# Modulation rows of both halves turned together, experts' weight pieces ending at banks, tokens gathered one expert at a time

## The chip, the cores and the metric

The kernel runs on one core of a Trainium2 chip. The metric is the device time of one execution in microseconds (us). Engines are named as in the profile: PE is TensorE's matmuls and PEld its loads of the stationary operand, DVE is VectorE, ACT is ScalarE, POOL is GpSimd, and SP issues most of the transfers.

## What is computed

The reference takes 256 tokens of width 1024 through two blocks of two layers each, all in float32. Two parts of it matter here. The first block modulates its activations by six rows per layer that come from the conditioning vectors:

```python
mod = silu_c @ ada_w[l] + ada_b[l]
modc = silu_cc @ ada_w[l] + ada_b[l]
sh1, sc1, g1, sh2, sc2, g2 = [m[:, None, :] for m in jnp.split(mod, 6, axis=-1)]
...
a = modulate(h, norm1_g[l], sh1, sc1)     # rmsnorm(h, g) * (1 + scale) + shift
```

The last layer of the second block is a mixture of 8 experts of hidden width 1408. Each token goes to its two best experts; an expert computes `(silu(h @ w1) * (h @ w3)) @ w2`, and the results are added with the router's weights.

## The kernel before

The weights, some 400 MB of float32, are read once, in the order in which they are used. `wload` (L225 to L236) moves a piece of up to 2048 columns by 128 rows into a buffer `raw` (SP issues the transfer at L225). It then handles sub-pieces of up to 1024 columns: ACT casts one to the rounded format fp32r, `whi` (L233), and DVE subtracts this from the raw piece to get the low part `wlo` (L236); in the experts' stage every sixth `wlo` is POOL's. The tokens are split in the same way (`xh`, `xl`; `gh`, `gl` for gathered tokens). A product of full precision is then three fp32r matmuls that add into one bank of 512 columns: `gemm_tok` issues high times high (L326), high times low (L327) and low times high (L328) for each group of 128 rows and each bank; such three are a triple below. The buffers are rings: a transfer waits until the slot it will fill has been read.

The experts' w1 and w3 have 1408 columns, which `cut` divides into banks of 512, 512 and 384. They are the only weights here wider than 1024, so for them `plan` lays 8 rows of 1408 end to end and cuts the whole at every 2048 columns, and `wload` at every 1024. These cuts fall inside banks, and a bank cut in two costs two triples of its row group.

The modulation's rows are made in `ada`, a generator that the kernel steps along between other work. For each layer, each of six rows s and each half h of 512 columns, PE computes the row (L509, a stationary operand of 32 columns), ACT copies the result from its bank to a tile `mod` (L516), and PE turns it from a row into a column per group of 128 features (L520): 8 matmuls whose stationary operand is every eighth column of `mod`, 64 columns in all, and whose moving operand is a selector of 2 columns (`c_sel`). In float32 each is two matmul instructions, so the trace has 16 in a run. DVE adds the bias and applies the norm's gain (L521, L524). There are 24 such halves. Those of the first two rows come first of all; while their weights arrive, `busy` (L473) fills PE's row with matmuls on zeros. The others are stepped in the background of the first block's GEMMs.

`moe` (L1700) first ranks the tokens of each expert, and splits the token state into `xth` and `xtl` (written at L373). `gather` (L1787) then makes a one-hot matrix `G` on DVE for two experts together (L1790, compared with a row of indices, `b_iota`). For each of 8 feature groups k it multiplies `G`, 256 columns wide, with every eighth column of `xth` and `xtl` (L1798), and the results are copied to `gh` by ACT and to `gl` by DVE (L1801). The first gather runs alone; the later ones are stepped in the background of the GEMMs, as are `weigh` (L1811, the weights of an expert's tokens, `cmb`), `turn` (L1831) and `scatter` (L1838). For an expert come w1, then the w2 of the expert before it, whose evacuation is `yh` and `yl` (L1862), then w3. A GEMM takes its banks from a ring of four.

Of the kernel before, what the change touches and what calls it, by code (L numbers as in the profile page):

```python
# [10 lines left out]
F32 = mybir.dt.float32  # L11
F32R = mybir.dt.float32r
# [3 lines left out]
OP = mybir.AluOpType  # L16
# [68 lines left out]
class Net:  # L85
# [134 lines left out]
    def wload(self, src, n, cw, f0):  # L220
# [5 lines left out]
        step = 1024 if len(src.shape) == 2 else 1024 // cw * cw  # L226
        out = []
        for c in range(0, n, step):
            m = min(step, n - c)
            s = raw[:, c:c + m]  # L230
# [7 lines left out]
            for k in range(a // cw, -(-(a + m) // cw)):  # L238
                o = k * cw - a
                out.append((k, max(0, -o), min(cw, m - o), *((lambda c, n, d=d, o=o: d[:, o + c:o + c + n]) for d in (hi, lo))))  # L240
        return out

    @staticmethod
    def plan(w, c0, cw):

        k, out = 0, []
        for view in w:
            nk = view.shape[1]
            if cw > 1024:
                flat = view.rearrange("p k n -> p (k n)")  # L250
                for f in range(0, nk * cw, 2048):
                    v = flat[:, f:min(f + 2048, nk * cw)]
                    out.append((repr(v), (v, v.shape[1], cw, k * cw + f)))
            else:
# [195 lines left out]
    def ada_setup(self):  # L450
        nc, a = self.nc, self.a
        self.zero = self.b1.tile([P, 512], BF16, name="zero")
        nc.vector.memset(self.zero, 0.0)
        self.ct = self.b1.tile([P, KD, 32], F32, name="ct")
# [14 lines left out]
    def busy(self, n):  # L469

        o = self.acc()
        for _ in range(n):
            self.tc.keep_in_program_order(self.nc.tensor.matmul(o, self.zero[:, :P], self.zero, start=True, stop=True))  # L473

    def ada_lambda(self):
# [4 lines left out]
        lqk = self.b1.tile([P, 2, 2, 64], F32, name="lqk")  # L480
# [12 lines left out]
    def ada(self, l, s, norm=None):  # L493
# [5 lines left out]
        self.mods[l, s] = o  # L499
        for h in range(2):  # L500
# [20 lines left out]
            nc.vector.tensor_tensor(out=o[rw], in0=pf[rw, :2 * KD].rearrange("p (k c) -> p k c", c=2),  # L521
                                    in1=self.adab[rw, l, s].unsqueeze(2).to_broadcast([64, KD, 2]), op=OP.add)
            if norm is not None:
# [1478 lines left out]
```

## Time and profile before

| | us |
|---|---|
| median of 3 runs | 2471.06 (2470.54 to 2473.48) |
| the profiled execution | 2465.78 |
| its span in the trace | 2464.3 |
| mean granted TensorE clock in it | 0.969 of full speed |
| busy in the span: PE, PEld, DVE, ACT, POOL | 2353.4, 1903.9, 1493.5, 1064.8, 299.0 |
| the experts' stage, first GEMM to last | 2000.9 to 2430.9 |

A busy share of the whole span says little here, since the stages have different limits: the page's slices show DVE between 2 and 8 tenths. Matmul records overlap their neighbours, as one is pipelined behind the other; the pace of PE is read from the starts of neighbours. The trace's instructions of `gemm_tok` in the experts' stage are known by `gh` and `gl`.

### The profile page before, as it was taken

What the parts mean: (1) busy time and instruction counts of PE and PEld (TensorE: products, weight loads), DVE (VectorE), ACT (ScalarE), POOL (GpSimd) and SP (SyncE); (2) the same over time, 40 slices, a digit from 0 to 9 for tenths busy, and PEclk for the clock granted to TensorE, in tenths of its full rate; (3) what the DMA queues carried; (4) which work ended last, traced back from release to release, by engine and by line L of the source; (5) the groups of instructions that cost most, each with busy time, mean ns of one, the idle gap of its engine ahead of it and who ended that gap; (6) DMA issues with size and microseconds to landing.
All of it is one profiled execution on the core that took longest, in us unless ns stands there. A gap on an engine that the chain in (4) does not pass through costs nothing.

```text
span 2464.3 us, 33187 instructions
## 1 busy us (share of the span) xinstructions
PE 2353.4 (95%) x13174; PEld 1903.9 (77%) x13174; DVE 1493.5 (61%) x2476; ACT 1064.8 (43%) x1684; POOL 299.0 (12%) x242
## 2 busy tenths in 40 slices
PE   8899999999998999999999989989999979999996
PEld 4567887777786778977887768868887778888885
DVE  4248732332356564568566765567566778897887
ACT  3137432222234544433343344423353447676773
POOL 1100000000002010003101210022101222222221
PEclk8899999999999999999999999999999989999998
DMA  8571244444323055544243444634343439888994
GB/s 296 150 201 52 88 151 144 159 166 163 107 81 123 10 200 164 196 147 156 84 160 130 154 165 148 215 111 143 102 161 120 155 129 346 292 327 288 328 337 159
DMA packets 121507, 419.45 MB, mean 170 GB/s; under 512 B 10992, under 2 KB 16112, under 8 KB 100352
## 3 DMA queue, kind: packets, MB, share of 16 engines
q1 hardware_dynamic: 114128, 401.32, 46.8%
q0 software_dynamic: 4832, 15.34, 2.3%
q8 instruction: 105, 1.72, 0.3%
q10 hardware_dynamic: 2384, 0.59, 0.1%
q14 instruction: 58, 0.48, 0.1%
HBM read 416.15 MB, written 1.07 MB: 169 GB/s over the span
## 4 chain that ended last, share of the span: by engine, by line
PE 84%; DVE 9%; issue 2%; ACT 2%; POOL 1%; DMA 1%; SPq 0%; ACTq 0%; POOLq 0%; DVEq 0%
PE acc L326 18%; PE acc L327 18%; PE acc L328 18%; PE acc L359 4%; PE acc L360 3%; PE acc L361 3%; DVE wlo L236 3%; PE mi L1032 2%; PE mi L520 2%; PE mi L509 2%; PE mi L1350 2%; PE mi L379 1%; PE mi L1798 1%; PE mi L988 1%; PE mi L1016 1%
## 5 line engine op out<-in xcount | busy, mean ns | idle before, releaser
L236 DVE TENSOR_TENSOR wlo<-raw,whi 128x1024 fp32r<-128x1024 f32 (+2 forms) x648 | 802.1, 1263 | 507.4 <-ACT whi L233 505.0
L233 ACT CAST whi<-raw 128x1024 fp32r<-128x1024 f32 (+2 forms) x692 | 673.0, 1010 | 741.5 <-PE acc L328 541.8
L326 PE MATMUL acc<-whi,xh 128*128 128x512 f32 (+3 forms) x1184 | 466.0, 397 | 18.6 <-ACT whi L233 12.4
L327 PE MATMUL acc<-wlo,xh 128*128 128x512 f32 (+3 forms) x1184 | 461.7, 390 | 11.9 <-DVE wlo L236 11.8
L328 PE MATMUL acc<-whi,xl 128*128 128x512 f32 (+3 forms) x1184 | 458.6, 388 | 3.4 <-DVE xl L373 3.4
L326 PEld LDWEIGHTS acc<-whi,xh 128*128 128x128 f32 x1184 | 227.9, 193 | 68.2 <-ACT whi L233 13.4
L327 PEld LDWEIGHTS acc<-wlo,xh 128*128 128x128 f32 x1184 | 227.8, 192 | 57.1 <-DVE wlo L236 19.8
L328 PEld LDWEIGHTS acc<-whi,xl 128*128 128x128 f32 x1184 | 227.7, 192 | 43.3 <-DVE xl L373 5.3
L326 PE MATMUL acc<-whi,hh 128*128 128x512 f32 x528 | 209.2, 396 | 0.0
L327 PE MATMUL acc<-wlo,hh 128*128 128x512 f32 x528 | 208.9, 396 | 0.0
L328 PE MATMUL acc<-whi,hl 128*128 128x512 f32 x528 | 208.4, 395 | 0.3 <-DVE hl L373 0.3
L326 PE MATMUL acc<-whi,gh 128*128 128x384 f32 (+3 forms) x512 | 172.8, 338 | 1.8 <-DVE yl L1862 1.8
L328 PE MATMUL acc<-whi,gl 128*128 128x384 f32 (+3 forms) x512 | 170.4, 333 | 0.0
L327 PE MATMUL acc<-wlo,gh 128*128 128x384 f32 (+3 forms) x512 | 170.3, 333 | 0.0
L236 POOL TENSOR_TENSOR wlo<-raw,whi 128x1024 fp32r<-128x1024 f32 x44 | 108.6, 2467 | 343.9 <-ACT whi L233 343.9
L359 PE MATMUL acc<-xh,whi 128*128 128x512 f32 (+1 forms) x384 | 147.4, 385 | 0.0
L360 PE MATMUL acc<-xl,whi 128*128 128x512 f32 (+1 forms) x384 | 146.0, 381 | 0.0
L361 PE MATMUL acc<-xh,wlo 128*128 128x512 f32 (+1 forms) x384 | 145.2, 379 | 0.0
L326 PEld LDWEIGHTS acc<-whi,hh 128*128 128x128 f32 x528 | 100.2, 190 | 26.4 <-issue 4.2
L328 PEld LDWEIGHTS acc<-whi,hl 128*128 128x128 f32 x528 | 100.2, 190 | 22.5 <-DVE hl L373 0.7
L327 PEld LDWEIGHTS acc<-wlo,hh 128*128 128x128 f32 x528 | 100.0, 189 | 21.2
L326 PEld LDWEIGHTS acc<-whi,gh 128*128 128x128 f32 x512 | 97.2, 190 | 11.2 <-DVE yl L1862 2.3
(578 smaller groups left out, 3242.6 us busy)
## 6 DMA issues: line engine op xcount, KB each, us to landing
raw<-in_exp_w_dram SPq DMA_DIRECT2D x120, 1024.0 KB, 6.6
raw<-in_ada_w_dram SPq DMA_DIRECT2D x48, 1024.0 KB, 5.3
raw<-in_w_in_dram SPq DMA_DIRECT2D x40, 1024.0 KB, 4.8
raw<-in_ffn_w_in_dram SPq DMA_DIRECT2D x32, 1024.0 KB, 5.0
raw<-in_ffn_w_dram SPq DMA_DIRECT2D x27, 1024.0 KB, 4.9
raw<-in_ffn_w_out_dram SPq DMA_DIRECT2D x19, 1024.0 KB, 5.0
raw<-in_exp_w_dram SPq DMA_DIRECT2D x24, 512.0 KB, 5.5
raw<-in_even_w_in_dram SPq DMA_DIRECT2D x10, 1024.0 KB, 5.5
```

The costliest lines, as they stand in the source:

```text
L233: nc.scalar.copy(hi, s)
L236: e.tensor_tensor(out=lo, in0=s, in1=hi.bitcast(F32), op=OP.subtract)
L326: nc.tensor.matmul(o, xh, hi(c, m), start=k == 0, stop=False)
L327: nc.tensor.matmul(o, xh, lo(c, m), start=False, stop=False)
L328: nc.tensor.matmul(o, xl, hi(c, m), start=False, stop=k == K - 1 and c + m == b + bw)
L359: nc.tensor.matmul(o, wh, xh[:, n0:n1], start=k == 0, stop=False)
L360: nc.tensor.matmul(o, wh, xl[:, n0:n1], start=False, stop=False)
L361: nc.tensor.matmul(o, wl, xh[:, n0:n1], start=False, stop=k == K - 1)
L509: nc.tensor.matmul(ps[32 * j:32 * j + 32, :], self.ct[:, 4 * g + j, :], v[:, j, :], start=g == 0, stop=g == 1, tile_position=(0, 32 * j))
L520: nc.tensor.matmul(pf[rw, 2 * k:2 * k + 2], mod[:, k::KD], self.sel2, start=True, stop=True, tile_position=(0, 64 * h))
L1032: nc.tensor.matmul(po[:, (h - c0) * 64:(h - c0) * 64 + 64], aT[:, j * P:(j + 1) * P], v(h, jj), start=jj == 0, stop=jj == nkb - 1)
L1350: nc.tensor.matmul(ps[t][rw, h * n:h * n + n], lhsT(m, rw), rhs(m, rw), start=True, stop=True, tile_position=(64 * (cl ^ t), 64 * (cl ^ t)))
```

## The change

`ends` is new: it lists the places where a bank of a row ends and picks of these, for each piece, the last one that keeps the piece at 2048 columns or less; `wload` does the same at 1024. Pieces of w1 and w3 become 1920 or 1792 columns wide, and sub-pieces 1024 or 896. There are 6 pieces per GEMM as before, and 12 sub-pieces where 11 were. In `ada` both halves go into one tile `mod` of 1024 columns, and one run of 8 matmuls with a stationary operand of 128 columns, still every eighth, turns them; DVE's instructions at the end are one pair in place of two. The small tensors of the modulation lie in a pool of their own (`ada`), with a zero tile of 128 columns in place of 512, which the fillers read four times over. In `moe` the layout of `xth` and `xtl` puts the columns of one k side by side, a gather is for one expert, in two steps of four k each, and the ring of raw weights has three more buffers there and not one more.

```diff
...
-        step = 1024 if len(src.shape) == 2 else 1024 // cw * cw
-        out = []
-        for c in range(0, n, step):
-            m = min(step, n - c)
-            s = raw[:, c:c + m]
+        step = 1024 // cw * cw
+        out, c = [], 0
+        for end in self.ends(n, cw, 1024, f0) if len(src.shape) == 2 else [min(i + step, n) for i in range(0, n, step)]:
+            m = end - c
+            s = raw[:, c:end]
...
+    def ends(cls, n, cw, most, f0=0):
+
+
+        edges = [r + b + w for r in range(0, f0 + n, cw) for b, w in cls.cut(cw)]
+        edges = [e - f0 for e in edges if f0 < e <= f0 + n]
+        out, at = [], 0
+        for e, after in zip(edges, edges[1:] + [None]):
+            if after is None or after - at > most:
+                out.append(e)
+                at = e
+        return out
...
-                for f in range(0, nk * cw, 2048):
-                    v = flat[:, f:min(f + 2048, nk * cw)]
+                f = 0
+                for e in cls.ends(nk * cw, cw, 2048):
+                    v = flat[:, f:e]
...
+        mod = self.ap.tile([P, D], F32, name="mod", tag="mod", bufs=1)
...
-            mod = self.sp.tile([P, 512], F32, name="mod", tag="xt", bufs=3)
-            nc.scalar.copy(mod, ps)
-            pf = self.mi()
-            rw = slice(64 * h, 64 * h + 64)
-            for k in range(KD):
-                nc.tensor.matmul(pf[rw, 2 * k:2 * k + 2], mod[:, k::KD], self.sel2, start=True, stop=True, tile_position=(0, 64 * h))
...
+            nc.scalar.copy(mod[:, h * 512:h * 512 + 512], ps)
+            if h == 0:
+                yield
+
+        pf = self.mi()
+        for k in range(KD):
+            nc.tensor.matmul(pf[:, 2 * k:2 * k + 2], mod[:, k::KD], self.sel2, start=True, stop=True)
...
-        self.extend(self.late, (pool, dict(raw=1)))
+        self.extend(self.late, (pool, dict(raw=3)))
...
-        xth, xtl = (pool.tile([P, 2, D], F32R, name=n) for n in ("xth", "xtl"))
+
+        xth, xtl = (pool.tile([P, 2, KD, P], F32R, name=n) for n in ("xth", "xtl"))
...
-                self.split(xth[:, t], xtl[:, t], self.x[:, t])
+                self.split(xth[:, t], xtl[:, t], self.x[:, t].rearrange("p (q k) -> p k q", k=KD))
...
-                for k in range(0, KD, 2):
+                gh, gl = gx[e] = [pool.tile([P, KD, P], F32R, name=n, tag=n, bufs=2) for n in ("gh", "gl")]
+                for k in range(0, KD, 4):
...
-                                nc.tensor.matmul(pg[:, j], x[:, t, k + j::KD], G[g][:, t].rearrange("p e s -> p (e s)"),
-                                                 start=t == 0, stop=t == 1)
+                                nc.tensor.matmul(pg[:, j], x[:, t, k + j], G[e][:, t], start=t == 0, stop=t == 1)
...
-                    if e % 2 == 0 and e + 2 < E:
-                        self.later(gather(e // 2 + 1))
+                    if e + 1 < E:
+                        self.later(gather(e + 1))
...
```

On PE, in the first w1 GEMM, where the second row group's piece ends (an order's row is line, operation, out<-in and shape; the lines of `gemm_tok` move from L326 to L342, of the gather from L1798 to L1817). Before:

```order
L326 MATMUL acc<-whi,gh 128x512
L327 MATMUL acc<-wlo,gh 128x512
L328 MATMUL acc<-whi,gl 128x512
L326 MATMUL acc<-whi,gh 128x128
L327 MATMUL acc<-wlo,gh 128x128
L328 MATMUL acc<-whi,gl 128x128
L326 MATMUL acc<-whi,gh 128x384
L327 MATMUL acc<-wlo,gh 128x384
L328 MATMUL acc<-whi,gl 128x384
L1798 MATMUL mi<-G,xth 128x256 x4
L1798 MATMUL mi<-G,xtl 128x256 x4
```

The same place after the change:

```order
L342 MATMUL acc<-whi,gh 128x512
L343 MATMUL acc<-wlo,gh 128x512
L344 MATMUL acc<-whi,gl 128x512
L342 MATMUL acc<-whi,gh 128x384
L343 MATMUL acc<-wlo,gh 128x384
L344 MATMUL acc<-whi,gl 128x384
L1817 MATMUL mi<-G,xth 128x128 x8
L1817 MATMUL mi<-G,xtl 128x128 x8
```

The triple of 128 columns, a bank's remainder, is gone, and the background gather has twice the matmuls at half the width.

On PE, from the last half of the second modulation row to the first GEMM of the kernel (`raw` and `ct` are the row's weights and conditioning). Before:

```order
L520 MATMUL mi<-c_sel_94,mod 64x2 x8
L379 MATMUL mi<-diag,z 128x128 x8
L509 MATMUL mi<-raw,ct 32x512 x8
L520 MATMUL mi<-c_sel_94,mod 64x2 x8
L326 MATMUL acc<-whi,xh 128x512
```

After:

```order
L490 MATMUL acc<-zero 128x512
L528 MATMUL mi<-raw,ct 32x512 x8
L540 MATMUL mi<-c_sel_100,mod 128x2 x8
L342 MATMUL acc<-whi,xh 128x512
L343 MATMUL acc<-wlo,xh 128x512
```

One run of turns, over 128 columns, stands where the second of two over 64 stood; the first half's has left its place.

On DVE, from the ranks (`rk`) to the first copy of gathered low parts. Before:

```order
L1745 SCALAR_TENSOR_TENSOR rk<-mi,sel 128x16
L373 TENSOR_TENSOR xtl<-xstate,xth 128x1024
L1790 TENSOR_SCALAR G<-b_iota,rk 128x128 x4
L1766 TENSOR_SCALAR e_16008<-e_16008 128x2
L1768 TENSOR_TENSOR cmb<-cmb,sel 128x16
L236 TENSOR_TENSOR wlo<-raw,whi 128x1024
L1801 CAST gl<-mi 128x512 x2
```

After:

```order
L1765 SCALAR_TENSOR_TENSOR rk<-mi,sel 128x16
L389 TENSOR_TENSOR xtl<-xstate,xth 128x1024
L1810 TENSOR_SCALAR G<-b_iota,rk 128x128 x2
L1787 TENSOR_SCALAR e_15866<-e_15866 128x2
L1789 TENSOR_TENSOR cmb<-cmb,sel 128x16
L236 TENSOR_TENSOR wlo<-raw,whi 128x1024
L1788 RECIPROCAL e_15866<-e_15866 128x2
L236 TENSOR_TENSOR wlo<-raw,whi 128x896
L1790 TENSOR_TENSOR cmb<-cmb,e_15866 128x16
L236 TENSOR_TENSOR wlo<-raw,whi 128x896
L1810 TENSOR_SCALAR G<-b_iota,rk 128x128 x2
L1819 CAST gl<-mi 128x512
```

Two more pieces of `wlo` and the second expert's `G` now stand ahead of the first copy `gl`.

## Rows read from the trace of the kernel before

**Rows 1.** Busy time by engine (instructions), granted clock and transfers, by stretch:

```profile
core 0: us, PE busy (x) PEld busy (x) DVE busy (x) ACT busy (x) POOL busy (x), PEclk, DMA share, GB/s
2000.90:2430.90 430.00, 426.40 (x2307) 379.91 (x2307) 359.49 (x341) 293.88 (x338) 103.36 (x42) 1.00 0.86 313
2080.00:2100.00 20.00, 20.00 (x121) 18.29 (x120) 19.50 (x22) 12.33 (x15) 4.87 (x2) 1.00 0.87 313
```

**Rows 2.** Waits from 1990 us on: engine and line, releaser, total us, times, longest:

```profile
PE mi L1798 <- DVE G L1790: 1.8, 1, 1.8
PE acc L326 <- DVE yl L1862: 1.8, 4, 0.5
...
SPq L225 <- DVE wlo L236: 320.2, 134, 4.6
```

**Rows 3.** PE's groups by shape, from 1990 us (busy us, mean ns, idle):

```profile
L326 PE MATMUL acc<-whi,gh 128*128 128x512 f32 x160 | 65.6, 410 | 0.0
...
L326 PE MATMUL acc<-whi,gh 128*128 128x384 f32 x160 | 56.8, 355 | 1.8 <-DVE yl L1862 1.8
...
L326 PE MATMUL acc<-whi,gh 128*128 128x256 f32 x96 | 27.6, 288 | 0.0
...
L326 PE MATMUL acc<-whi,gh 128*128 128x128 f32 x96 | 22.8, 238 | 0.0
```

**Rows 4.** PE's timeline in two expert GEMMs: start, duration in us, instruction:

```profile
2003.16 0.22 PE L326 MATMUL acc<-whi,gh 128*128 128x128 f32 x1
...
2003.44 0.39 PE L326 MATMUL acc<-whi,gh 128*128 128x384 f32 x1
2003.67 0.34 PE L327 MATMUL acc<-wlo,gh 128*128 128x384 f32 x1
...
2418.08 0.39 PE L326 MATMUL acc<-whi,gh 128*128 128x512 f32 x1
...
2418.77 0.34 PE L326 MATMUL acc<-whi,gh 128*128 128x384 f32 x1
...
2419.30 0.28 PE L326 MATMUL acc<-whi,gh 128*128 128x256 f32 x1
...
2419.65 0.28 PE L326 MATMUL acc<-whi,gh 128*128 128x256 f32 x1
```

**Rows 5.** Loads of the stationary operand by shape, whole span:

```profile
L326 PEld LDWEIGHTS acc<-whi,gh 128*128 128x128 f32 x512 | 97.2, 190 | 11.2 <-DVE yl L1862 2.3 <-DVE gs L1922 0.3
...
L520 PEld LDWEIGHTS mi<-c_sel,mod 128*64 128x64 f32 x384 | 48.0, 216 | 11.9 <-ACT mod L516 10.1 <-issue 1.7
...
L1798 PEld LDWEIGHTS mi<-G,xtl 128*128 128x128 f32 x64 | 17.2, 338 | 0.0
...
L1350 PEld LDWEIGHTS mi<-TT,M 64*64 64x64 f32 x320 | 10.2, 135 | 0.7 <-issue 0.7
```

**Rows 6.** The chain of waits at the start and at the experts': start, us, what:

```profile
13.49 2.01 PE mi L520 x16
...
41.54 0.43 PE acc L328
...
1992.81 7.97 PE mi L1798 x32
```

**Rows 7.** DVE's timeline behind the ranks:

```profile
1993.21 1.22 DVE L236 TENSOR_TENSOR wlo<-raw,whi 128x1024 fp32r<-128x1024 f32 x1
...
1995.61 0.69 DVE L1801 CAST gl<-mi 128x512 fp32r<-128x512 f32 x1 [1.18 <-PE mi L1798]
```

**Rows 8.** Granted clock (third number from the end), in stretches as in rows 1:

```profile
41.00:46.60 5.60, 5.60 (x14) 4.40 (x15) 5.46 (x17) 3.58 (x10) 0.00 (x0) 0.50 0.74 248
112.80:118.80 6.00, 6.00 (x29) 4.52 (x32) 0.87 (x2) 0.24 (x1) 1.02 (x3) 0.72 0.52 175
611.10:617.10 6.00, 6.00 (x27) 5.13 (x27) 0.17 (x1) 0.00 (x0) 0.00 (x0) 0.72 0.97 328
1980.00:1999.20 19.20, 10.68 (x50) 9.78 (x51) 14.65 (x27) 4.31 (x10) 5.75 (x3) 0.50 0.00 1
```

More of the change, by code (lines that the diff above doesn't have):

```diff
@@ L240, in wload, with plan @@
                 out.append((k, max(0, -o), min(cw, m - o), *((lambda c, n, d=d, o=o: d[:, o + c:o + c + n]) for d in (hi, lo))))
+            c = end
         return out
-    @staticmethod
-    def plan(w, c0, cw):
+    @classmethod
+    def ends(cls, n, cw, most, f0=0):
[7 more added lines that the diff above has]
+        return out
+    @classmethod
+    def plan(cls, w, c0, cw):
         k, out = 0, []
@@ L472, in busy @@
         for _ in range(n):
-            self.tc.keep_in_program_order(self.nc.tensor.matmul(o, self.zero[:, :P], self.zero, start=True, stop=True))
+            self.tc.keep_in_program_order(self.nc.tensor.matmul(o.rearrange("p (j n) -> p j n", j=4), self.zero, self.zero.unsqueeze(1).to_broadcast([P, 4, P]),
+                                                                    start=True, stop=True))
     def ada_lambda(self):
@@ L1783, in experts, with gather @@
             G, gx, st = {}, {}, {}
-            def gather(g):
-                G[g] = self.xp.tile([P, 2, 2, P], F32R, name="G", tag="xp", bufs=4)
+            def gather(e):
+                G[e] = self.xp.tile([P, 2, P], F32R, name="G", tag="xp", bufs=4)
                 for t in range(2):
-                    for e in range(2):
-                        nc.vector.tensor_scalar(out=G[g][:, t, e], in0=iota, scalar1=rkb[:, t, 2 * g + e:2 * g + e + 1],
-                                                scalar2=None, op0=OP.is_equal)
-                gh, gl = gx[g] = [pool.tile([P, KD, 256], F32R, name=n, tag=n, bufs=2) for n in ("gh", "gl")]
-                for k in range(0, KD, 2):
+                    nc.vector.tensor_scalar(out=G[e][:, t], in0=iota, scalar1=rkb[:, t, e:e + 1], scalar2=None, op0=OP.is_equal)
+                gh, gl = gx[e] = [pool.tile([P, KD, P], F32R, name=n, tag=n, bufs=2) for n in ("gh", "gl")]
+                for k in range(0, KD, 4):
                     for i, (x, d) in enumerate(((xth, gh), (xtl, gl))):
-                        pg = self.mi().rearrange("p (k n) -> p k n", k=2)
-                        for j in range(2):
+                        pg = self.mi().rearrange("p (k n) -> p k n", k=4)
+                        for j in range(4):
                             for t in range(2):
-                                nc.tensor.matmul(pg[:, j], x[:, t, k + j::KD], G[g][:, t].rearrange("p e s -> p (e s)"),
-                                                 start=t == 0, stop=t == 1)
+                                nc.tensor.matmul(pg[:, j], x[:, t, k + j], G[e][:, t], start=t == 0, stop=t == 1)
                         if i:
-                            nc.vector.tensor_copy(d[:, k:k + 2], pg)
+                            nc.vector.tensor_copy(d[:, k:k + 4], pg)
                         else:
-                            nc.scalar.copy(d[:, k:k + 2], pg)
+                            nc.scalar.copy(d[:, k:k + 4], pg)
                     yield
             def weigh(e):
-                Gf = lambda t: G[e // 2][:, t, e % 2].bitcast(F32)
+                Gf = lambda t: G[e][:, t].bitcast(F32)
                 pc = self.mi()
@@ L1964, in block1 @@
             ctxs = cxp.tile([P, 2, D], F32, name="ctxs")
-            self.ada_setup()
             with tc.tile_pool(name="zx", reuse_waits="tile", side="right", bufs=1) as self.zp:
-                self.block1_layer0(ctxs)
+                with tc.tile_pool(name="ada", reuse_waits="tile", bufs=1) as self.ap:
+                    self.ada_setup()
+                    self.block1_layer0(ctxs)
                 self.store("h0", [self.x[:, 0], self.x[:, 1], ctxs[:, 0], ctxs[:, 1]])
```

29 lines of the change are left out of this document (15 added, 14 removed).

## The prediction

> **What bounds the kernel now.** I started with the time by stretch, since a share over the whole span mixes stages, and then read what ended TensorE's waits. In the experts' stage, 430 us long, PE is busy for 426.4 [rows 1], and from 1990 us to the end its largest kinds of wait are 1.8 us each, for a G and for a bank that yl frees; none is for a DMA or a split of weights [rows 2]. DVE is busy for 359.5 of the 430, and the SP queue stands 320.2 us waiting for a buffer of raw weights that DVE has to finish with [rows 1, 2]: weights arrive before PE wants them. So the stage is as long as PE's own instructions, and what the change takes off PE there comes off the end. The modulation's turns (L520) interrupt PE in the first 650 us, where PE also sets the pace; the first of them is on the chain that ended last [rows 6], and so are the next three. PE's pace is not its busy time, as its records overlap; I use starts of neighbours [rows 4].
>
> **A. Experts' weights end at banks.** One weight column group costs three matmuls. By their starts a triple is 0.69 us at 512 columns (2418.08 to 2418.77), 0.53 at 384 (2418.77 to 2419.30), 0.35 at 256 (2419.30 to 2419.65), and 0.28 at 128 (2003.16 to 2003.44), after which the first step of the next triple takes 0.23 (2003.44 to 2003.67) and not 0.18; so 0.33 with what it does to its neighbour [rows 4]. A 128-wide step is no cheaper than a 256-wide one, 0.11 to 0.12 each. The w1 and w3 GEMMs hold 160, 160, 96 and 96 triples of 512, 384, 256 and 128 [rows 3]: 160 x 0.69 + 160 x 0.53 + 96 x 0.35 + 96 x 0.33 = 260.5 us. Cut at banks of 512, 512 and 384, the same 16 GEMMs of 8 rows need 256 x 0.69 + 128 x 0.53 = 244.5. **-16.0.** With 0.28 instead of 0.33 it is -11.2, with 0.35 for the rarer follower -17.5. Casts and subtractions come in 12 sub-pieces per GEMM rather than 11; 16 more starts on ACT and DVE lie under PE, with DVE at 84% [rows 1]. Should that cover fail, rival 2 has the price. The number of DMAs stays 6 per GEMM.
>
> **B. Gather per expert.** Before, four gathers of 32 matmuls of 256 columns; the first steps at 7.97 / 32 = 0.249 us [rows 6]. That is the load of the stationary operand: 338 ns where its columns lie eight floats apart, against 190 where they are neighbours [rows 5]. A matmul of 256 columns behind a plain load steps at 0.12 [rows 4]. After, the copy xth/xtl is laid out with neighbours together, and there are 256 matmuls of 128 columns at a plain 0.115 or so: 29.4 us against 31.9. **-2.5.** Of this the first gather, on the path alone, goes from 7.97 to 3.7 us; the seven others cost 25.8 against 23.9. (The Trainium skill, "TensorE: Matmul & The Clock Gate", section "Back-to-back issue gap", gives about 81 ns per matmul at 128 columns; 256 of them would be an estimated 20.7 us, 8.7 less. The rows of this case, 0.11 at 128 and 0.23 at 512, lie above its figures, and the rows decide.) Bounds -5 to +1, by 0.105 and 0.13 per step.
>
> **C. The start of the experts' stage.** A gl copy takes DVE 0.69 us, and the one wlo piece ahead of the first of them 1.22; in between DVE waited for PE [rows 7]. After, three wlo pieces and four G stand ahead of the first gl copy; counted through from 1992.3 by these durations it ends near 1997.5. PE is done with 32 short matmuls and the four of L1772 near 1996.9, and the first two steps of the GEMM don't read gl: **+0.4**, bounds 0 and 2.5 (ACT's casts hold the wlo pieces back). The granted clock is 0.50, the 1.2 GHz level, until 1999.2, where PE was busy for 10.7 of 19.2 us [rows 8]. GEMM steps moved ahead into that stretch take 0.43 and not 0.23, as between 41.0 and 46.6 us at that level [rows 6, 8]: from 1996.9 to about 2000.1 that loses **+1.5**, bounds 0 (the clock comes up as early as the work) and 4 (some 8 us behind the GEMM's start).
>
> **D. Third bank.** PE waits four times, 1.8 in all, for the bank that yl has to free [rows 2]. It comes to that bank one 128-wide triple, 0.33, sooner: **+1.3**, bounds 0 and 3.
>
> **E. Strided split.** For xth and xtl the state is now read eight floats apart, a pass that is on the chain and as wide as a wlo piece of 1.22 [rows 7]; I take its time to stay with its elements, **+0.2**, up to 1.2 if the stride doubles it.
>
> **F. The modulation's rows turned together.** Before, 24 runs of 16 matmuls (384 loads [rows 5]), 2.01 us each [rows 6]: 48.2. After, 12 runs of 16, each loading 128 columns eight apart instead of 64. What that load costs no row shows for plain f32, but rows 5 hold the neighbours: 64 columns 216 ns apart against 135 together, 128 columns 338 against 190. A column that is apart costs (338 - 216) / 64 = 1.9 ns, and in both apart forms the step is some 0.09 shorter than the load (0.126 for 216, 0.249 for 338). So I take 0.249: 12 x 16 x 0.249 = 47.8. **-0.5** with fewer entries. It halves the runs and doubles each: the gain of joining is eaten by the stride. Bounds: 0.12 a step is rival 1; at the whole load, 0.338, it would be +16.7, which I leave out since neither form steps at its load. The first two units are on the path: four runs of 2.01 before [rows 6], two of 4.0 after. If PE's row sets the time there, that is nothing; if the weights' arrival does, the last L509 end where they did and the last turn takes 4.0 for 2.0: **+0.8**, bounds 0 and 1.9.
>
> After some runs the granted clock falls to 0.50 for 3.4 us: the 6 us from 112.80 and from 611.10, each from the start of a run, have a mean of 0.72, which is 6 x 0.28 / 0.50 = 3.4 us at 0.50 [rows 8]. They are the first and the last of eight such falls behind the 20 runs after the first two units. At 0.43 a step for 0.23 one costs 3.4 x (1 - 0.23 / 0.43) = 1.6 us, all eight 12.6. In a run PE streams 2 columns a matmul; after, there are 10 runs of 4 us, and I expect more of them to be followed by a fall. I take nine: **+1.5**, bounds -6 (four) and +6 (twelve).
>
> **The rest at nothing.** Three more raw buffers and a small pool instead of a large one let transfers go earlier; PE waits on none [rows 2], and for a gain there is no wait to remove. Fillers (L473 to L490) stay 512 columns by broadcast. A few conversion inputs change places on SP: within 1 us either way.
>
> **Sum.** -16.0 - 2.5 + 0.4 + 1.5 + 1.3 + 0.2 - 0.5 + 0.8 + 1.5 = -13.3, against the profiled execution's 2465.78: 2452.5. This run lies 5.3 us under the median of 2471.06 and the sum is a difference, so I predict 2471.06 - 13.3 = **2458**. Ends that go together (A from -11 to -17.5, B, C, F's falls) give 2451 to 2464.
>
> **Rivals.**
> 1. *The load goes by columns alone.* Then the joined turn costs what one half did: 12 x 2.01 = 24.1, 23.6 less than in F, **2434**. Against it: the pairs of rows 5 and the gather's 0.249 step, slow with the same layout. For it: those pairs also differ in number format or size, and no row shows 128 f32 columns apart. (The Trainium skill states this rule, "TensorE: Matmul & The Clock Gate", section "LDWEIGHTS (loading the stationary operand)": the time is columns over 1.2 per ns, with no word on stride. By that 128 columns take 107 ns anywhere; the trace disagrees, 190 and 338 ns. Its page "SBUF — State Buffer", section "Specifications (TRN2)", asks for two hits in each 16-byte line, which columns 32 bytes apart miss.) Chance 0.10.
> 2. *Weights become the bound.* At 2080 DVE is busy 19.5 of 20 us; DMA's share over the stage is 0.86 [rows 1]. A PE that is 4% faster asks 4% more of both. If in half the stage it then waits for wlo, half of A and B goes: 2458 + 9 = **2467**. For it: this stretch; against it: the SP queue's 320.2 us of waiting for slots, a queue that is ahead on average, and DVE at 359.5 of some 414, 87%, in the shorter stage. Chance 0.12.
> 3. *Slower by the clock.* The place: behind the 10 later turns, each now 4 us in which PE streams 2 columns a matmul. If two falls follow each, or one that lasts twice as long, there are 20 for 8, 12 x 1.6 = +19 in place of +1.5: **2476**. It turns the sum's sign from some 17 falls (nine more than before, 14.8 us). For it: eight falls already behind 2 us runs. Against it: none of the 20 runs had two, and the work around them is full of 512-wide matmuls. Chance 0.06.
> 4. *The cuts don't do what they say*, A at nothing: the order shows that they do. Chance 0.01.
>
> **How the numbers follow.** The forecast has 0.71. What a measurement can tell here is about 0.2%, 4.9 us, so faster means below 2466.1. The forecast's cases are nearly all below it, rival 1 is, of rival 2 half. Faster: 0.69 + 0.10 + 0.05 = 0.84; same 0.02 + 0.07 + 0.01 = 0.10; slower 0.06. The range leaves out rivals 1, 3 and 4, 0.17: it goes from 2447, a little below the forecast's own end for terms that all fall well, to 2467, rival 2.
>
> **What would show it.** A: the records of L342 hold 256 of 512 and 128 of 384 and none of 128 or 256, and the stage from its first GEMM on is 14 to 17 us shorter, with PE's waits for wlo still under 3 us. B and C: 32 gather matmuls in 3.5 to 4 us, first GEMM near 1997 on the old axis, clock up near 2000. F: each turn (L540) 3.8 to 4.0 us; 2.0 would make rival 1 right. Falls behind turns: 7 to 11; 16 or more would make rival 3 right. The forecast is wrong if PE waits for wlo or whi for over 5 us in the stage, or if the turn's step is not near 0.25.

## The result, and the profile after

The changed kernel takes 2447.04 us (median of 4 runs, 2444.91 to 2448.38), the one before 2470.8 beside it: ratio 0.9906, 95% interval 0.9889 to 0.9924, so 19 to 27 us faster. The forecast was 2458, its range 2447 to 2467. The direction was right, the size 1.8 times what was forecast, and the time lies on the lower edge of the range. The profiled execution took 2447.04 us too. That of before took 2465.78, 5 us below its median; from trace to trace the change is 18.7 us, and this is what stages can explain.

The experts' stage, from the first to the last GEMM, first in the kernel before (the same columns as rows 1), then after. The last matmul of the last GEMM before starts at 2442.0, so the 430.0 us of [rows 1] stop 11 us short of the stage; PE is as full in the whole of it.

```profile
2001.00:2442.00 441.00, 437.40 (x2354) 388.79 (x2353) 364.83 (x344) 297.47 (x342) 105.77 (x43) 1.00 0.84 305
```

```profile
1994.20:2423.60 429.40, 425.59 (x2096) 363.14 (x2097) 355.57 (x353) 300.09 (x360) 115.23 (x46) 0.99 0.84 307
```

The stage is 11.6 us shorter and PE still fills it. It starts 6.7 us earlier; 5.6 of these are won before 676 us, where the last of the modulation's rows has been made. The waits of PE in the stage after (line, releaser, total us, times, longest) are as small as before, compare [rows 2]. Again none is for a split of weights (`hl` is a split of an expert's hidden values, `cw` a small copy of its tokens' weights):

```profile
PE acc L344 <- DVE hl L389: 2.2, 1, 2.2
PE acc L342 <- DVE yl L1879: 1.1, 1, 1.1
PE mi L1849 <- DVE cw L1831: 0.5, 1, 0.5
```

PE's groups in the stage after, which answer [rows 3]; the remainders of 256 and 128 columns are gone, and the triples number 256 and 128 as counted:

```profile
L342 PE MATMUL acc<-whi,gh 128*128 128x512 f32 x256 | 104.4, 408 | 0.0
...
L342 PE MATMUL acc<-whi,gh 128*128 128x384 f32 x128 | 43.6, 341 | 1.1 <-DVE yl L1879 1.1
```

The loads of a turn, which answer the L520 row of [rows 5]: 128 columns eight floats apart take 333 ns, much as xth's and xtl's did before.

```profile
L540 PEld LDWEIGHTS mi<-c_sel,mod 128*128 128x128 f32 x192 | 46.6, 333 | 5.3 <-ACT mod L534 4.8
```

The chain at the start of the stage after (start, us, what), which answers [rows 6]: the first gather is on it with 7.13 us, where 7.97 stood, and the first GEMM's steps take 0.43 where those of [rows 4] take 0.23:

```profile
1984.35 1.90 DVE xtl L389
1986.50 7.13 PE mi L1817 x32
1993.63 0.76 PE mi L1793 x4
...
1995.44 0.43 PE acc L344
```

### The profile page after: what moved, and what is told of

Its sections match the earlier page's. It is cut to its first block, busy times and chain, and to the rows that moved or that the text cites. A ratio compares the mean times of both kernels' runs of the same rounds, so it can differ in the third digit from the quotient of the medians.

```text
span 2445.3 us, 32300 instructions
## 1 busy us (share of the span) xinstructions
PE 2338.9 (96%) x12726; PEld 1878.7 (77%) x12726; DVE 1483.7 (61%) x2473; ACT 1067.6 (44%) x1700; POOL 307.6 (13%) x245
## 4 chain that ended last, share of the span: by engine, by line
PE 86%; DVE 9%; issue 2%; POOL 1%; ACT 1%; DMA 1%; SPq 0%; POOLq 0%; ACTq 0%; DVEq 0%
PE acc L342 19%; PE acc L343 19%; PE acc L344 18%; PE acc L375 4%; PE acc L376 3%; PE acc L377 3%; DVE wlo L236 2%; PE mi L1052 2%; PE mi L528 2%; PE mi L540 2%; PE mi L1370 2%; PE mi L395 1%; PE mi L1008 1%; PE mi L1817 1%; PE mi L1036 1%
## 5 line engine op out<-in xcount | busy, mean ns | idle before, releaser
L236 DVE TENSOR_TENSOR wlo<-raw,whi 128x1024 fp32r<-128x1024 f32 (+3 forms) x661 | 797.3, 1233 | 517.9 <-ACT whi L233 512.4
L233 ACT CAST whi<-raw 128x1024 fp32r<-128x1024 f32 (+5 forms) x708 | 674.4, 992 | 723.0 <-PE acc L344 522.0
L342 PE MATMUL acc<-whi,xh 128*128 128x512 f32 (+3 forms) x1184 | 468.3, 398 | 11.6 <-ACT whi L233 4.8
L342 PEld LDWEIGHTS acc<-whi,xh 128*128 128x128 f32 x1184 | 228.6, 193 | 65.1 <-issue 12.2
L342 PE MATMUL acc<-whi,hh 128*128 128x512 f32 x528 | 209.3, 396 | 0.0
L236 POOL TENSOR_TENSOR wlo<-raw,whi 128x1024 fp32r<-128x1024 f32 (+1 forms) x47 | 118.0, 2511 | 325.7 <-ACT whi L233 325.7
L342 PE MATMUL acc<-whi,gh 128*128 128x512 f32 (+1 forms) x384 | 147.4, 386 | 1.1 <-DVE yl L1879 1.1
L344 PE MATMUL acc<-whi,gl 128*128 128x512 f32 (+1 forms) x384 | 145.2, 378 | 0.0
L343 PE MATMUL acc<-wlo,gh 128*128 128x512 f32 (+1 forms) x384 | 144.8, 377 | 0.0
L342 PEld LDWEIGHTS acc<-whi,hh 128*128 128x128 f32 x528 | 100.2, 190 | 26.6 <-issue 3.4
L375 PEld LDWEIGHTS acc<-xh,whi 128*128 128x128 f32 x384 | 73.9, 193 | 28.5 <-ACT whi L233 6.7
```

What stands on the lines that cost most here:

```text
L233: nc.scalar.copy(hi, s)
L236: e.tensor_tensor(out=lo, in0=s, in1=hi.bitcast(F32), op=OP.subtract)
L342: nc.tensor.matmul(o, xh, hi(c, m), start=k == 0, stop=False)
L343: nc.tensor.matmul(o, xh, lo(c, m), start=False, stop=False)
L344: nc.tensor.matmul(o, xl, hi(c, m), start=False, stop=k == K - 1 and c + m == b + bw)
L375: nc.tensor.matmul(o, wh, xh[:, n0:n1], start=k == 0, stop=False)
```

## The experiments

All ran beside the kernel before; the intervals are for the ratio to it. What they were to tell apart: the change has four parts (cuts at banks, gather, joined turns, raw buffers), and their sum had come out some 10 us better than forecast by the medians.

**The cuts alone.** The hunks of `wload`, `plan` and `ends`, nothing else.

```diff
-        step = 1024 if len(src.shape) == 2 else 1024 // cw * cw
...
+        for end in self.ends(n, cw, 1024, f0) if len(src.shape) == 2 else [min(i + step, n) for i in range(0, n, step)]:
```

> The kernel before with only the experts' pieces cut at banks. Step A of the prediction: 16 us less in triples, of which 1 to 2 come back at the bank that yl frees, so 13 to 15 us faster than before, no triple of 128 or 256 columns left, and PE's waits for wlo in the experts' stage under 3 us. Rival 2 (weights become the bound): half of that, 7 to 9 us, with waits for wlo or whi of over 5 us.

Measured: 2478.72, ratio 1.0042 (1.0027 to 1.0056), 7 to 14 us slower than before. Both expectations were wrong, even in sign. The trace says where. The stage takes 450.3 us for 441.0; its first 106 us are full, and after that PE idles 18 of 344 us, with DVE busy 85% of that time (83% of the stage before) and the transfers' share below that of the full part:

```profile
2004.20:2110.00 105.80, 105.80 (x501) 92.08 (x501) 89.28 (x96) 74.53 (x90) 27.64 (x11) 1.00 0.88 320
2110.00:2454.50 344.50, 326.50 (x1469) 265.56 (x1468) 292.85 (x262) 223.19 (x268) 92.33 (x35) 1.00 0.83 293
```

PE's waits are the ones that rival 2 named, for the low parts:

```profile
PE acc L343 <- POOL wlo L236: 9.2, 10, 1.7
PE acc L343 <- DVE wlo L236: 6.4, 10, 1.2
```

**The gather alone**, with the new layout of xth and xtl:

```diff
-                                nc.tensor.matmul(pg[:, j], x[:, t, k + j::KD], G[g][:, t].rearrange("p e s -> p (e s)"),
-                                                 start=t == 0, stop=t == 1)
+                                nc.tensor.matmul(pg[:, j], x[:, t, k + j], G[e][:, t], start=t == 0, stop=t == 1)
```

> The kernel before with only the gather for one expert at a time and the new layout of xth and xtl (raw ring as before). By the prediction's steps B, C and E about 0.4 us faster. By the trace of the changed kernel, where the first gather's 32 matmuls of 128 columns took 7.1 us at the 1.2 GHz level and the later ones 0.108 each, against 0.240 for 256 columns before: 0.8 us less in the first, 1.9 more in the seven others, 0.8 more in the split of xtl, and up to 2.2 lost as the first GEMM starts at the 1.2 GHz level: 2 to 4 us slower.

Measured: 2473.85, ratio 1.0018 (1.0006 to 1.003), 1 to 7 us slower. Its experts' stage takes 445.6 us for 441.0, so the reading of the changed kernel's trace held and the prediction's small gain did not.

**The joined turns alone**, with the small pool and the smaller zero tile that come with them:

```diff
-            for k in range(KD):
-                nc.tensor.matmul(pf[rw, 2 * k:2 * k + 2], mod[:, k::KD], self.sel2, start=True, stop=True, tile_position=(0, 64 * h))
...
+        for k in range(KD):
+            nc.tensor.matmul(pf[:, 2 * k:2 * k + 2], mod[:, k::KD], self.sel2, start=True, stop=True)
```

> The kernel before with only the modulation's halves turned together (and its small tensors in a pool of their own). Step F of the prediction: 1.8 us slower. By the trace of the changed kernel, which was 5.7 us ahead at 700 us (turns 44 us in all for 48, a stall of 8.9 us near 81 us gone, more time at the 1.2 GHz level behind the turns): 5 to 7 us faster, with 45 to 55 us at that level between 60 and 700 us. Rival 3's clock loss would show as that time at the lower level.

Measured: 2459.09, ratio 0.9957 (0.9942 to 0.9972), 7 to 14 us faster. Its trace is 5.8 us shorter than that of before, 4.5 of it won in the first 700 us; its experts' stage is the same 441.0. The medians give 11.3, since the trace of before is of a short execution. Between 60 and 700 us the granted clock is at 0.50 for 51 us, as the expectation had it from the changed kernel, against 38 before.

**Turns with their columns side by side**, otherwise the changed kernel:

```diff
-        mod = self.ap.tile([P, D], F32, name="mod", tag="mod", bufs=1)
+        mod = self.ap.tile([P, KD, P], F32, name="mod", tag="mod", bufs=1)
...
-            nc.scalar.copy(mod[:, h * 512:h * 512 + 512], ps)
+            nc.scalar.copy(mod[:, :, 64 * h:64 * h + 64], ps.rearrange("p (q k) -> p k q", k=KD))
...
-            nc.tensor.matmul(pf[:, 2 * k:2 * k + 2], mod[:, k::KD], self.sel2, start=True, stop=True)
+            nc.tensor.matmul(pf[:, 2 * k:2 * k + 2], mod[:, k], self.sel2, start=True, stop=True)
```

> The changed kernel, but ACT writes the tile mod so that the 128 columns of a turn lie side by side. If the load's price is the distance of its columns (the prediction's step F), a turn of 16 falls from 3.6 to about 1.8 us, 12 x 1.8 = 22 us less, and with short turns fewer falls of the clock follow, 3 to 8 us more: 22 to 30 us faster than the changed kernel. If a load goes by its number of columns alone (rival 1), the turn stays at 3.6 us and nothing is gained.

Measured: 2413.79, ratio 0.9778 (0.9761 to 0.9795), 33 us faster than the changed kernel. The load of a turn, and a turn on PE's timeline:

```profile
L540 PEld LDWEIGHTS mi<-c_sel,mod 128*128 128x128 f32 x192 | 23.5, 195 | 5.7 <-ACT mod L534 4.8
```

```profile
350.17 1.84 PE L540 MATMUL mi<-c_sel,mod 128*128 128x2 f32 x16
351.88 0.48 PE L376 MATMUL acc<-xl,whi 128*128 128x512 f32 x1
```

The same 128 columns load in 195 ns for 333, and a turn takes 1.71 us (350.17 to 351.88) where it took 3.6: rival 1 is refuted by the one thing that was changed. (The Trainium skill's rule by columns alone, "TensorE: Matmul & The Clock Gate", section "LDWEIGHTS (loading the stationary operand)", has no word on where the columns lie; the 107 ns estimated by it for 128 columns agree with neither load.) ACT pays nothing for writing `mod` with a stride: its 24 copies have a median of 586 ns with it as without. Twelve turns shorter by 1.9 us make some 23 of the 33 us. I put the rest down to the clock, whose granted level did not fall once from 86 to 755 us:

```profile
86.00:755.00 669.00, 657.21 (x3277) 506.98 (x3275) 317.35 (x664) 237.88 (x423) 25.35 (x43) 1.00 0.43 137
```

**One more raw buffer for three**, in the changed kernel:

```diff
-        self.extend(self.late, (pool, dict(raw=3)))
+        self.extend(self.late, (pool, dict(raw=1)))
```

> The changed kernel with one more raw buffer in the experts' stage, as before, and not three. If the cuts at banks need the deeper ring (alone, with one more buffer, they made the kernel slower, and PE waited 15.6 us for wlo), then the time is about that of the joined turns alone and the losses of the two others, 2459.1 + 8.3 + 3.5 = 2471, and at least 2460, with over 10 us of PE's waits for wlo. If the raw buffers do nothing, as the prediction has it, 2447.

Measured: 2444.53, ratio 0.9911 (0.9898 to 0.9923). Its runs and those of the changed kernel overlap: the raw buffers do nothing that can be told, as the prediction had it, and the explanation of the first experiment by them fell.

**The changed kernel without the cuts** (the first experiment's hunks taken back):

```diff
-        for end in self.ends(n, cw, 1024, f0) if len(src.shape) == 2 else [min(i + step, n) for i in range(0, n, step)]:
...
+        step = 1024 if len(src.shape) == 2 else 1024 // cw * cw
```

> The changed kernel with the pieces of 2048 and 1024 columns of before, and the three more raw buffers. If these serve the cuts at banks alone, nothing is gained from them here, since PE did not wait before: 2459.1 + 3.5 = 2462.6, and the cuts are worth 15.6 us beside them, step A of the prediction. If the deeper ring has a gain of its own, the time lies nearer to 2447 than to 2463.

Measured: 2464.57, ratio 0.9984 (0.9976 to 0.9993). So beside the gather per expert the cuts are worth 17.5 us, and alone they cost 8. Its stage is 445.6 us for 429.4 after, 16.2 more, and PE fills it as it does after:

```profile
1995.50:2441.10 445.60, 442.00 (x2480) 392.78 (x2481) 364.09 (x340) 298.07 (x344) 104.87 (x43) 0.99 0.82 296
```

**Gather for two experts with the new layout**, on the kernel with flat turns and with one more raw buffer:

```diff
+            def gather(g):
...
+                                nc.tensor.matmul(pg[:, j], x[:, t, k + j], G[g][:, t].rearrange("p e s -> p (e s)"),
+                                                 start=t == 0, stop=t == 1)
```

> As e4_flat, but tokens are gathered for two experts together, with the new layout of xth and xtl. The larger gathered tokens leave room for one more raw buffer only. 128 gather matmuls of 256 columns at some 0.12 us would take 15 us for 28: by PE's own work 12 us faster than e4_flat, 2402. If the ring of raw weights bounds the experts' stage with one more buffer, the gain doesn't come and the loss of e1_ends does: 2420 to 2440, with over 10 us of waits for wlo.

Measured: 2424.58, ratio 0.9829 (0.9815 to 0.9842), 11 us slower than e4_flat. The time is within the second expectation, but its reason, the raw ring, was gone with e5_raw1. What e1_ends and this one share, both slower than their own work on PE says, is the cuts together with a gather for two.

**Fillers ahead of the first gather:**

```diff
                 last.append(pre(t))
+            self.busy((8, 24)[t])
...
+        self.busy(8)
         rk = pool.tile([P, 2, E], F32, name="rk")
```

> As e4_flat, with 8, 24 and 8 filler matmuls of 512 columns (their result is not used) on PE while it waits for the split of the tokens and for G ahead of the first gather. If the first gather is slow for the 1.2 GHz level (0.22 a step for 0.11 later) and the first GEMM's steps too (0.43 for 0.23), the clock is up when the gather starts: 3.5 and 2.2 us less, and up to 1 elsewhere, so 2407 to 2409 for 2413.8. If the first gather is slow for another reason (G, or its copies), nothing changes, or the fillers delay the router by 1 us.

Measured: 2411.68, ratio 0.9778 (0.9764 to 0.9792), no difference that can be told. It is no answer to the question: the granted clock was up from 1937.2 to 1947.4 and down again in the gather, behind 4 us in which PE was busy for 2.0 (columns as in rows 1, the granted clock third from the end).

```profile
1945.00:1949.00 4.00, 2.04 (x15) 1.77 (x12) 2.52 (x10) 2.96 (x6) 0.00 (x0) 0.80 0.00 0
1949.00:1952.50 3.50, 3.50 (x11) 1.48 (x10) 3.37 (x7) 0.00 (x0) 0.00 (x0) 0.50 0.00 0
1952.50:1959.00 6.50, 6.50 (x33) 6.50 (x32) 6.02 (x12) 1.17 (x2) 0.00 (x0) 0.50 0.60 221
```

**The paired gather's steps spread over two experts' w1:**

```diff
-                    if e % 2 == 0 and e + 2 < E:
-                        self.later(gather(e // 2 + 1))
+                    if e + 2 - e % 2 < E:
+                        if e % 2 == 0:
+                            gx["half"] = gather(e // 2 + 1)
+                        self.later(islice(gx["half"], 2) if e % 2 == 0 else gx.pop("half"))
```

> As e7_pair, but the four steps of the gather for the next two experts are stepped two beside the w1 of one expert and two beside that of the next. In e1_ends and e7_pair the split weights that lie ready for PE run down to nothing in the stretch after the first gathers that stand four steps in a row beside one w1, and don't come back; with two steps per w1 (the changed kernel) they never do. If it is the crowding of ACT's and DVE's copies that drains them, PE doesn't wait for wlo here and the 12 us of shorter gathers show: 2401 to 2404. If it is the larger matmuls, the tiles or the one raw buffer, it stays at 2424.

Measured: 2425.99, ratio 0.9834 (0.9817 to 0.9851), the second case of the expectation. The crowding is not it.

**The same with fillers in every gap:**

```diff
                 last.append(pre(t))
+            self.busy((8, 36)[t])
...
             nc.tensor.matmul(lg[:, t], l, fold, start=True, stop=True)
+            if t:
+                self.busy(6)
...
+        self.busy(9)
         rk = pool.tile([P, 2, E], F32, name="rk")
```

> As e9_spread, with fillers on PE ahead of the first gather in all the gaps that e8_fill left: 36 while the tokens are split, 6 behind the router and 9 ahead of the first gather. In e8_fill the granted clock came up at 1937.2 us, fell again at 1947.4, where PE did next to nothing for 4 us, and the gather ran at the 1.2 GHz level as without fillers. If the level is what made the first gather and GEMM slow, they now run at 2.4 GHz: 3.5 + 2.2 us less than e9_spread, some 2396 to 2399. If the clock falls all the same, nothing.

Measured: 2424.86, ratio 0.9832 (0.9816 to 0.9848). The end did not move, but the stretch did. The granted clock of the 12 us around the first gather, in e9_spread and here:

```profile
1945.00:1957.00 12.00, 7.84 (x38) 7.38 (x39) 8.75 (x23) 4.37 (x9) 0.00 (x0) 0.50 0.00 0
```

```profile
1945.00:1957.00 12.00, 10.94 (x80) 7.86 (x79) 10.91 (x26) 5.23 (x10) 0.70 (x1) 1.00 0.01 1
```

The gather takes 4.26 us for 6.64, and the stage starts 1.8 us earlier though the trace was 1.3 behind before it: 3.1 won, and lost again in the stage, where PE waits 20.0 us for wlo, and 19.0 in e9_spread.

**The spread gather on the kernel before, with the cuts**, that is the edits of e1_ends and of e9_spread:

```diff
+        for end in self.ends(n, cw, 1024, f0) if len(src.shape) == 2 else [min(i + step, n) for i in range(0, n, step)]:
...
+                        self.later(islice(gx["half"], 2) if e % 2 == 0 else gx.pop("half"))
```

> The kernel before with the pieces cut at banks, as e1_ends, and the four steps of a gather stepped two beside each w1, as in e9_spread; layout, width and turns as before. If the crowded copies are what cost e1_ends its gain, step A shows here: 14 to 16 us faster than before, 2454 to 2457, with no waits for wlo. If e1_ends lost to something else in the cuts, it stays at 2470 to 2479.

Measured: 2480.45, ratio 1.0052 (1.0036 to 1.0068). The same verdict, on the kernel of before.

**ACT's order held.** The waits of ACT in e10_spread_fill show what the slow kernels have in common. (`GT`, `yh`, `gs`, `hh` and `gh` are ACT's copies of results that PE has made.) From 2100 to 2380 us, engine and line, releaser, total us, times, longest:

```profile
ACT yh L1888 <- PE acc L345: 25.6, 5, 6.1
ACT GT L1846 <- PE mi L1844: 21.6, 4, 7.1
...
ACT gs L1941 <- PE acc L345: 11.1, 5, 5.1
ACT hh L387 <- PE mi L1858: 10.7, 8, 3.4
```

ACT stands in front of a copy of something that PE has not made yet, for up to 7 us, and behind that copy are the whi casts that the next wlo are made from. The first experiment's kernel does the same. From 2250 to 2450 us, where 14.5 of its 15.6 us of waits for wlo lie:

```profile
ACT GT L1835 <- PE mi L1833: 19.9, 4, 7.1
ACT yh L1877 <- PE acc L344: 15.0, 3, 5.9
ACT gs L1928 <- PE acc L344: 13.2, 3, 5.1
```

In the kernel before, all such waits from 2100 to 2380 us come to 0.3 us. In e4_flat, in a stretch of 280 us too, ACT hardly waits for such a copy; there it waits until PE has read a slot that the next cast can fill:

```profile
ACT whi L233 <- PE acc L344: 68.4, 70, 2.2
ACT whi L233 <- issue: 10.2, 10, 2.2
ACT GT L1837 <- PE mi L1835: 1.0, 5, 0.2
```

So I counted, in each trace, how many columns of weights ACT has cast ahead of each GT copy in its own order, less those that PE had used ahead of the matmul that the copy reads. There is one number per expert, worked out from the traces; the first 512 columns that PE uses in the stage are left out, so the stock itself is 512 smaller throughout:

```
before           5632 6656 6656 6656 6656 6656 6656 6656
e2_gather        5632 6656 6656 6656 6656 6656 6656 6656
after            5248 5248 5248 5248 5248 5248 5248 5632
e1_ends          5248 4352 4352 2304 2432  896 2432 2560
e7_pair          5248 4352 4352 2304 2432  896 2432 2560
e10_spread_fill  5248 4352 3328 2304 2432  896 2432 2560
```

This order is made when the kernel is built, and runs as it stands. The last experiment changes the order in e10_spread_fill and not the work: pieces are fetched, cast and subtracted three ahead in the program, and ACT's copies come behind the last cast issued.

```diff
+            if self.look and self.behind is None:
+                for key, args in list(self.plan(w, c0, cw))[i + 1 + len(self.ahead):i + 1 + self.look]:
+                    self.ahead.append((key, self.wload(*args)))
...
+    def edge(self):
+        return self.tc.issue_after(self.cast.ins) if self.look and self.behind is None else ExitStack()
...
-                        with self.tc.high_priority(offset=PRI):
+                        with self.tc.high_priority(offset=PRI), self.edge():
                             evac(t, b, bw, ps[t, b][:, :bw])
...
-                self.step(self.bgn * sum(cb - ca for _, ca, cb, *_ in mine) / 2048 / len(toks))
+                with self.edge():
+                    self.step(self.bgn * sum(cb - ca for _, ca, cb, *_ in mine) / 2048 / len(toks))
```

> As e10_spread_fill, with ACT's order in the experts' stage held: whi casts are issued three pieces ahead, and what ACT does for a result of PE (gs, yh, hh, gh, GT) comes behind the last cast issued. In the traces of e1_ends, e7_pair and e9_spread the casts that stand ahead of such an instruction in ACT's order shrink from 5248 columns beyond what PE has used by then, at the first expert, to 900 to 2600 at the sixth; in the kernel before and in the changed one they stay at 5200 to 6700. Here they stay at 5200 to 6700 by the order. If this lead is what the cuts and the paired gather lose, PE waits for wlo less than 3 us, and the time is e4_flat's 2413.8 less 12 for the gathers and 3 for the clock at the first one: 2398. If ACT, DVE or the transfers can't supply PE at this pace whatever the order, it stays at 2425.

Measured: 2407.95, ratio 0.9751 (0.9728 to 0.9774), 17 us faster than the same kernel without the order by the medians, 20 by the ratios. Its count is 6144 for every GT copy but the last, 6656. The stage in e10_spread_fill and in e12_lead:

```profile
1957.10:2401.50 444.40, 422.09 (x1970) 345.98 (x1969) 382.20 (x357) 296.31 (x358) 122.18 (x46) 1.00 0.84 304
```

```profile
1960.50:2384.40 423.90, 415.34 (x1970) 347.26 (x1969) 371.54 (x357) 298.22 (x358) 121.81 (x46) 1.00 0.87 318
```

PE idles 8.6 us in it for 22.3, its waits for wlo are 3.4 for 20.0, and the stage is 20.5 shorter. The largest waits that are left:

```profile
PE mi L1868 <- DVE cw L1850: 4.0, 1, 4.0
PE acc L352 <- DVE wlo L237: 2.8, 7, 0.7
```

So beside a gather for two, the order of the feeding work is most of what the cuts lost. As the edit also moves transfers and subtractions ahead, not ACT's casts alone, how much of it is ACT's order by itself is not shown. That the same holds in e1_ends, whose count shrinks and whose ACT waits alike, is inferred and was not run. It did not give the 27 us expected: 3.4 us of waits for low parts and one of 4.0 for a small copy on DVE remain in the stage, and it starts 3.4 us later than in e10_spread_fill, behind a first part that the edit leaves as it was. It is the fastest kernel measured here by its median; its interval overlaps that of e4_flat.

## Why the prediction was right or wrong, point by point

**A, the cuts: the size right, one condition not seen.** Forecast -16.0; the stage without the cuts is 445.6 and with them 429.4, -16.2. Triples counted and priced by neighbours' starts carry. But I treated the parts as a sum. The cuts alone are 8 us slower, and rival 2 at 0.12 was not a small worry but what is seen without the new gather. I looked at DVE's share and the queue's stock for it, and DVE's share does not tell the kernels apart: 83% of the stage before, 83% after, 85% of the part of e1_ends in which PE waits. What does is how much casting stands ahead of a few copies in ACT's order. That the order counts beside a gather for two is shown by e12_lead; for e1_ends it is inferred. I could have compared it ahead of the result, as I did on DVE for one copy. That the change came with the gather that doesn't lose by the cuts was luck.

**B, the gather: wrong.** Forecast -2.5. The step that failed is "a plain 0.115 or so" for all 256 matmuls. The prices in [rows 4] are from a stretch at 2.4 GHz, and the first gather runs at 1.2: there a matmul of 128 columns behind a plain load steps at 7.13 / 32 = 0.22 us, so 0.8 us was won and not 4.3. The later ones do go at 0.108 (8 in 0.84 to 0.89 us):

```profile
2001.80 1.00 PE L1817 MATMUL mi<-G,xth 128*128 128x128 f32 x8
2002.64 1.06 PE L1817 MATMUL mi<-G,xtl 128*128 128x128 f32 x8
2003.53 0.45 PE L342 MATMUL acc<-whi,gh 128*128 128x512 f32 x1
```

As 7 x 32 x 0.108 = 24 us they cost about what the wide ones did. e2_gather shows the part as a loss. In e10_spread_fill a gather for two with plain loads makes 8 matmuls of 256 columns in 0.94 us, half the time per expert; it came to nothing as long as the stock of casts shrank.

**C, the start: right in kind.** The copy of gl made no wait. The first GEMM ran at the 1.2 GHz level from 1994.2 to 1999.1, 4.9 us at 0.43 for 0.23, which loses 2.3; the forecast was 1.5 for this and 0.4 for the copy. The stretch before was busier than in [rows 8], 15.1 of 19.1 us, and the level was still 0.50:

```profile
1980.00:1999.10 19.10, 15.13 (x61) 13.81 (x60) 12.73 (x31) 4.77 (x9) 0.00 (x0) 0.50 0.41 151
```

**D, the third bank: not there.** PE waits 1.1 us for yl, less than before; other small waits took its place (hl 2.2), and the sum stayed at some 3.8. That B, C and D together cost the stage 4.6 us (445.6 without the cuts for 441.0) where 1.9, 1.5 and 1.3 were forecast is partly luck.

**E, the strided split: mis-sized.** On the chain it takes 1.90 us for 1.13, +0.8 where I took 0.2, inside its bound.

**F, the turns: wrong in sign.** Forecast +1.8; measured -5.6 by the trace, 7 to 14 us faster as a part. Three terms:
- A turn takes 3.6 to 4.0 us, 0.225 to 0.25 a step where 0.249 was priced, and 12 of them 43.8 us for 48.2. That is -4.4 for -0.5.
- Nine falls of the clock follow the turns, the very number I took. But they are longer: five of 3.4 us, three of 6.8 and one of 10.2, so PE is at 0.50 for 47.6 us there, against 27.2 in eight falls of 3.4 before. The 9.1 us from 365.30 below have a mean of 0.63, which is 6.7 us at 0.50. Part of it costs nothing, since a turn at that level takes no longer: the one at 365.31, in which the level falls, takes 3.60 us, and the one at 632.01, where it doesn't, 3.60. Beside the turns' -4.4 and the -6.8 of the next point, some 5.5 is left of the -5.6 for the falls, an estimate where the forecast had 1.5: rival 3's "one that lasts twice as long" is partly what happened.

```profile
365.31 3.73 PE L540 MATMUL mi<-c_sel,mod 128*128 128x2 f32 x16
368.91 0.78 PE L376 MATMUL acc<-xl,whi 128*128 128x512 f32 x1
...
632.01 3.74 PE L540 MATMUL mi<-c_sel,mod 128*128 128x2 f32 x16
635.61 0.47 PE L377 MATMUL acc<-xh,wlo 128*128 128x512 f32 x1
```

```profile
365.30:374.40 9.10, 9.10 (x30) 7.94 (x30) 0.40 (x2) 0.60 (x1) 0.00 (x0) 0.63 0.67 230
```

- A term was missing. Near 81 us PE waited 8.8 us for a cast whose raw weights came late, and 2.0 after (1.2 and 0.8). The waits of PE from 78 to 92 us, before and after:

```profile
PE acc L326 <- ACT whi L233: 8.8, 1, 8.8
```

```profile
PE acc L342 <- ACT whi L233: 1.2, 1, 1.2
PE acc L343 <- DVE wlo L236: 0.8, 1, 0.8
```

I had put other transfers past each other at the start "within 1 us either way"; that sentence failed. What counts is when the wait ends. The first matmul behind it, in the kernel before, after, and in e4_flat (the idle time ahead of it in brackets):

```profile
90.14 2.07 PE L326 MATMUL acc<-whi,xh 128*128 128x512 f32 x4 [8.78 <-ACT whi L233]
```

```profile
83.01 0.50 PE L342 MATMUL acc<-whi,xh 128*128 128x512 f32 x1 [1.17 <-ACT whi L233]
```

```profile
80.96 0.80 PE L342 MATMUL acc<-whi,xh 128*128 128x512 f32 x1 [6.53 <-ACT whi L233]
```

In e4_flat PE waits longer since it gets there sooner. In all kernels whose halves are turned together, e3_ada with 84.3 among them, the wait ends between 81 and 84.4 us; in the four whose halves are turned one by one it ends between 89.5 and 92.7. So these 7 us come with the edit of e3_ada. Whether the joined turns, the small pool or the order of the transfers does it was not tried and stays open.

**The median.** I moved the sum onto the median of before, since it is a difference. That run's 5 us are part of the 23.8; the runs of before in all comparisons lie between 2461 and 2473.5, those of the changed kernel within 4 us. Where these 12 us come from is open too, but the length of the wait near 81 us is not it. Up to the token split the kernels before, e1_ends, e2_gather and e11_ends_spread issue the same matmuls in the same order; in their traces the stage starts at 2001.0, 2004.2, 2004.7 and 2005.1 us, nearly all of the difference is there by 140 us, and this wait is 8.8, 8.2, 8.1 and 8.4 us long.

**What it comes to.** By trace: -5.6 to 676 us, -0.7 up to the first gather, -0.4 in it, -11.6 in the stage, -0.6 behind it: -18.9 of the span's -19.0, rounded. The forecast's -13.3 has the stage right (about -11 of it: A, C's clock, D and the seven later gathers) and the modulation's part wrong. That the time still lies in the range is luck: its lower edge was set for terms of the forecast that all fall well, and what brought the time there is largely a wait that the sum had at nothing, and a median that lies 5 us above the trace.

## What to carry to other kernels

An operand that PE loads is best written so that its columns lie side by side: in this kernel ACT could do it for nothing, and that was worth more than the whole change. Before parts of a change are added up, compare, on each engine that feeds the bound one, how much feeding work stands ahead of each copy that waits for the bound engine; in the kernels here where that lead shrank from expert to expert, a gain in PE's own work turned into waits. And a price read at one clock level isn't the price at the other: here the step behind a plain load went from 0.108 to 0.22 us, that of a turn, whose columns lie apart, stayed at 0.225.

## What was not expected of the hardware

- Matmuls of 128 columns behind plain loads of 128 step at 0.108 us at 2.4 GHz and 0.22 at 1.2 GHz. With columns eight floats apart the first gather of before stepped at 0.249 at 1.2 GHz, and the turns after at 3.60 / 16 = 0.225 whether the level fell within them or not.
- Falls of the granted clock behind the turns after the first two units: none behind the ten of 1.7 to 1.9 us in e4_flat, eight behind the 20 of 2.0 us before, nine behind the ten of 3.6 us or more after, four of them longer than 3.4 us. The rows show this of these runs and no more.
- ACT writes `mod` with a stride in the same 586 ns as without, and the turns get 1.9 us shorter each.
